# Moving modulation sums, partition sums and a gelu in a one-core hybrid mixer and expert kernel

## The chip, the cores and the metric

One core of one Trainium2 chip runs the whole program. The metric is device time in microseconds from the start to the end of one execution, the lower the better. The time before is 1646.16 us, the median of 3 runs (1645.67 to 1648.39).

## The reference, cut to what matters

One layer over 1024 latent tokens and 256 context tokens of width 1024, in float32. Modulation vectors come from the conditioning vector; four of the six are needed late (gain 1, shift 2, scale 2, gain 2):

```
mod_x = silu(c) @ w_mod + b_mod          # six vectors of 1024
hx = rmsnorm(x, norm1_g) * (1 + sc1x) + sh1x
u, v, xx, g = split(hx @ w_in)           # 512 columns each
rec = gelu(g) * (recurrence of xx, both directions)
sgu = gelu(u) * (spatial mix, per 128 positions, of rmsnorm(gelu(v)))
x = x + g1x * (concat(sgu, rec) @ w_out)
hx2 = rmsnorm(x, norm2_g) * (1 + sc2x) + sh2x
x = x + g2x * expert_choice_ffn(hx2, w_router, w1, w3, w2)   # 16 experts, 128 tokens each
out = rmsnorm(x, final_g)
```

## The kernel before, in words

Every float32 matmul is done as three matmuls on operands split into a rounded part (`hi`, copied by ACT) and its rest (`lo`, subtracted by DVE). The program order written in the file is the order of each engine's queue, and of the load queue of SP.

The stages in order: modulation vectors and x transposed (up to line 502); the recurrence (631 to 680); v and the spatial gate (830 to 875); the output projection with the second norm and the router, tile by tile of 128 tokens (1069 to 1164); selection of tokens by sorting (1168 to 1205); 16 experts (1320 to 1378); the last norm.

**Late modulation vectors.** `mod_rows` (line 396) adds one row block of `w_mod` (128 rows by 1024 columns, 512 KB) times the conditioning value into an accumulator on DVE (line 402 for the first of a vector, line 404 for the other seven). Thirty-two such blocks, eight to a vector, pass through a ring of three buffers; each call then issues the load of the block three further on (`mod_load`, line 389, on SP), which may write only when DVE has read that buffer. `mod_cols` (line 408) sums the accumulator over the 128 partitions with 16 thin matmuls (line 412; the trace counts 16 for 8 written ones) and DVE adds the bias (line 413). The order of vectors is gain 1, scale 2, shift 2, gain 2. The accumulator and the ring lie in two of the twelve 1 MB buffers that the expert weights use later.

**v.** `v_mm(t, h)` (line 754) is 24 matmuls of 256 columns. Tiles 0 to 3 do half 0 first and half 1 in the loop of line 849; tiles 4 to 7 do both in the loop of line 865. `v_evac` (line 766) is a gelu and four squares with row sums on ACT. `v_norm` (line 774) needs the sums of four tiles and scales those tiles on DVE. `spatial_mm` (783) multiplies by the spatial weights on PE, `spatial_ew` (788) applies gain, bias and u on DVE.

**w_out.** Four 1 MB loads in two halves (`load_wo`, 807) through two buffers; `scale_wo` (815) multiplies by gain 1 on DVE, `split_wo` (822) makes `hi` on ACT and `lo` on DVE. Half 1 meets the recurrence, half 0 the spatial gate. The loads of half 0 wait until the subtractions of half 1 have read their buffers.

**Output tiles.** `out_mm(t, h)` (921) is 24 matmuls of 512 columns into two PSUM banks. Before the loop of line 1075, `row_bcast` (732) spreads scale 2 and shift 2 over the partitions: eight transposes on PE for each vector, in two banks each. There are eight PSUM banks, handed out again in about the order in which they come free. In the loop, for tile t: the softmax of the router for t-2, the residual and norm for t-1, `out_mm(t)`, the transposes of `router_t(t-1)` (990), `fill(20)` (941: sorting steps on DVE, where there are any), the next spatial tile, the router product for t-1.

**Expert weights.** `load_next` (84) issues 1 MB loads on SP ahead of use; the first use is at line 1150, behind output tile 7.

Of the kernel before, what the change touches and what calls it, by code (L numbers as in the profile page):

```python
# [11 lines left out]
AF = mybir.ActivationFunctionType  # L12
# [33 lines left out]
def hybrid_layer(ctx, tc, x, c, ctxt, c_ctx, w_mod, b_mod, norm1_g, norm2_g, w_in, sgu_g, sgu_w,  # L46
# [3 lines left out]
    V, A, PE, G = nc.vector, nc.scalar, nc.tensor, nc.gpsimd  # L50
# [19 lines left out]
    def bank(shape, name, small=0):  # L70
        return banks[small].tile(shape, F32, name=name, tag="bk")

    def raw(shape, dt, name):
        return rawp.tile(shape, dt, name=name, tag="raw")

    def raw2(shape, dt, name):
        n = shape[1] // 2
        return Two([raw([shape[0], n] + shape[2:], dt, name) for _ in range(2)], n)
# [5 lines left out]
    def load_next(n=1, queue=nc.sync):  # L84
        for _ in range(n):
            which, w, e, u = pieces.pop(0)
            q, h = divmod(u, 2)
            r = 4096 // w.shape[2]
            t = raw([P, 2048], F32, "raw")
            src = w[e, q * P * r:(q + 1) * P * r, :].rearrange("(p k) f -> p (k f)", p=P)  # L90
            queue.dma_start(t, src[:, h * 2048:(h + 1) * 2048])
            units.append(((which, e, u), t))
# [296 lines left out]
    def mod_load():  # L389
        n = nload[0]  # L390
        if n < len(todo):
            g, k = todo[n]
            nc.sync.dma_start(ring[:, n % 3], w_mod[k * P:(k + 1) * P, (2 + g) * D:(3 + g) * D])
            nload[0] += 1

    def mod_rows(cnt=1):
        for _ in range(cnt):
            n = ndone[0]
            k = todo[n][1]
            macc, row = ring[:, 3], ring[:, n % 3]  # L400
            if k == 0:
                V.tensor_scalar(macc, row, cs[:, k, 0:1], None, op0=OP.mult)
            else:
                V.scalar_tensor_tensor(macc, row, cs[:, k, 0:1], macc, op0=OP.mult, op1=OP.add)  # L404
            ndone[0] += 1
            mod_load()

    def mod_cols():
        g = todo[ndone[0] - 1][0]
        p = bank([P, 8, 2], "pm")  # L410
        for j in range(8):
            PE.matmul(p[:, j], ring[:, 3, j * P:(j + 1) * P], ones, start=True, stop=True)
        V.tensor_tensor(mcol[:, g], p[:, :, 0], prmT[:, 32 + 8 * g:40 + 8 * g], op=OP.add)
# [92 lines left out]
    uT = pu.tile([P, 4, S], F32, name="uT")  # L506
# [225 lines left out]
    def row_bcast(dst, col, view=lambda p: p):  # L732
        for h in range(2):
            p = bank([P, 512], "rb")
            for j in range(4):
                PE.transpose(p[:, j * P:(j + 1) * P],
                             col[:, 4 * h + j:4 * h + j + 1].to_broadcast([P, P]), ident)
            A.activation(dst[h] if isinstance(dst, list) else dst[:, h * 512:(h + 1) * 512], view(p), AF.Copy)  # L738
# [15 lines left out]
    def v_mm(t, h):  # L754
        if h == 0:
            PV[t] = bank([P, 512], "pv")
        hi, lo = hxT[t // 4]
        ts = slice((t % 4) * P, (t % 4 + 1) * P)
        o = PV[t][:, h * 256:(h + 1) * 256]
        for k in range(8):  # L760
            wh, wl = wv[h][k]
            PE.matmul(o, hi[:, k, ts], wh, start=(k == 0), stop=False)
            PE.matmul(o, hi[:, k, ts], wl, start=False, stop=False)
            PE.matmul(o, lo[:, k, ts], wh, start=False, stop=(k == 7))

    def v_evac(t):
        p = PV.pop(t)
        A.activation(gv[:, t], p, AF.Gelu_apprx_tanh)
        junk = psp.tile([P, 512], F32, name="junk2", tag="bk")
        for h in range(4):  # L770
            A.activation(junk[:, h * P:(h + 1) * P], gv[:, t, h * P:(h + 1) * P], AF.Square,
                         accum_out=vst[:, 0, 4 * t + h:4 * t + h + 1])
# [34 lines left out]
    def load_wo(h):  # L807
        return [(k, load_wo2(h, k)) for k in (0, 2)]
# [6 lines left out]
    def scale_wo(h, ts):  # L815

        for k, t in ts:
            for n in range(2):
                v = t[:, :, n * 512:(n + 1) * 512]
                V.tensor_tensor(v, v, g1row[n][:, None, :].to_broadcast([P, 2, 512]), op=OP.mult)  # L820

    def split_wo(h, ts):
        wo[h] = (raw2([P, 4, D], F32R, "woh"), raw2([P, 4, D], F32R, "wol"))
        hi, lo = wo[h]
        for k0, t in ts:
            for k in range(2):
                A.activation(hi[:, k0 + k], t[:, k], AF.Copy)
                V.tensor_sub(lo[:, k0 + k], t[:, k], hi[:, k0 + k])
# [19 lines left out]
    wor1 = load_wo(1)  # L848
    for t in range(4):
        v_mm(t, 1)  # L850
        if t == 0:
            mod_cols()
        if t == 1:
            scale_wo(1, wor1)
        v_evac(t)
        mod_rows(1)
    V.scalar_tensor_tensor(a2c, mcol[:, 2], 1.0, prmT[:, 96:104], op0=OP.add, op1=OP.mult)
    split_wo(1, wor1)
    wor0 = load_wo(0)
    mod_rows(4)  # L860
    for b in range(4):
        A.activation(uT[:, b], uT[:, b], AF.Gelu_apprx_tanh)
    A.preload_act_table_set("natural_log_exp_and_others")
    v_norm(0)
    for t in range(4, 8):
        for h in range(2):
            v_mm(t, h)
        v_evac(t)
        if t == 5:
            scale_wo(0, wor0)  # L870
        if t == 6:
            mod_cols()
    for t in range(3):
        spatial_mm(t)
    spatial_ew(0)
# [26 lines left out]
    def x_load(t):  # L902
        XR[t] = pe_.tile([P, D], F32, name="xr", bufs=2)
        nc.sync.dma_start(XR[t], x[t * P:(t + 1) * P])

    x_load(0)
    x_load(1)
    load_next(2)
    affs = tv[:, :, :, 1]

    groups = ((0,), (1, 2), (3, 4), (5,), (6, 7))
# [9 lines left out]
    def out_mm(t, h, ks=range(4), ns=(0, 1)):  # L921
        ts = slice(t * P, (t + 1) * P)
        if t not in PW:
            PW[t] = [bank([P, 512], "pw") for _ in range(2)]
        yh, yl = (recT[0][:, :, ts], recT[1][:, :, ts]) if h else YH[t]
        pw = PW[t]
        wh, wl = wo[h]
        for k in ks:
            st_, en = h == 1 and k == 0, h == 0 and k == 3
            for n in ns:  # L930
                PE.matmul(pw[n], yh[:, k], wh[:, k, n * 512:(n + 1) * 512], start=st_, stop=False)  # L931
            for n in ns:
                PE.matmul(pw[n], yh[:, k], wl[:, k, n * 512:(n + 1) * 512], start=False, stop=False)  # L933
            for n in ns:
                PE.matmul(pw[n], yl[:, k], wh[:, k, n * 512:(n + 1) * 512], start=False, stop=en)  # L935
# [5 lines left out]
    def fill(n=1):  # L941

        for _ in range(n):
            if fills and not callable(fills[0]) and done2[0] >= fills[0]:
                fills.pop(0)
            if fills and callable(fills[0]):
                fills.pop(0)()
            if fills2:
                fills2.pop(0)()
                done2[0] += 1  # L950
# [39 lines left out]
    def router_t(t, hs=(0, 1)):  # L990
        hx2 = H2[t]
        if t not in HT:
            HT[t] = pe_.tile([P, 8, P], F32, name="hxT2")
        for h in hs:
            p = bank([P, 4, P], "ht")
            for k in range(4):
                PE.transpose(p[:, k], hx2[:, (4 * h + k) * P:(4 * h + k + 1) * P], ident)
            A.activation(HT[t][:, 4 * h:4 * h + 4], p, AF.Copy)
# [68 lines left out]
        q_bitonic(32, m, dst, f)  # L1067

    out_mm(0, 1)
    row_bcast(A2, a2c)  # L1070
    row_bcast([qkp(SH2, 0, 2), qkp(SH2, 2, 2)], mcol[:, 1], lambda p: qpk(p, 0, 2))
    out_mm(1, 1)
    out_mm(0, 0)
    spatial_mm(3)
    for t in range(1, 8):
        if t > 1:
            router_sm(t - 2)
        if t == 2:
            q_sort(0, LS[0])
        if t in (4, 6):  # L1080
            i = t // 2 - 1
            q_sort(i, L1)
            q_merge(LS[1 - i % 2], L1, LS[i % 2])
        norm2_a(t - 1)
        if t + 2 < 8:
            spatial_ew(t + 2)
        if t == 7:
            break
        if t > 1:
            out_mm(t, 1, (0, 1))  # L1090
            router_w(t - 2)
            out_mm(t, 1, (2, 3))
        norm2_b(t - 1)
        y_split(t + 1)
        out_mm(t, 0)
        x_load(t + 1)
        if t == 1:
            spatial_mm(t + 3)
        router_t(t - 1)
        fill(20)  # L1100
        if t == 5:
            load_next(2)
        if t > 1 and t + 3 < 8:
            spatial_mm(t + 3)
        router_mm(t - 1)
# [404 lines left out]
```

## Time and profile before

| | |
|---|---|
| median of 3 runs | 1646.16 us |
| the profiled execution | 1644.65 us |
| its span, first to last instruction | 1642.6 us |
| mean granted TensorE clock | 0.967 of full |
| PE busy | 1537.4 us, 94% |
| DVE busy | 1385.6 us, 84% |
| ACT busy | 1090.2 us, 66% |
| POOL busy | 143.2 us, 9% |
| the chain that ended last, by engine | PE 69%, DVE 13%, DMA 7%, ACT 7%, issue 4% |

A timeline row gives the start in us from the start of the span, the duration, the engine, the source line, the operation, what is written and read, and how many instructions are merged in the row (xN). Brackets at the end hold the time for which the engine had been idle ahead of it, and what released it. SP rows are issues of loads and stores; an issue that lasts long was waiting. A clock of 1.00 is 2.4 GHz, 0.50 is 1.2 GHz.

### The profile page before, as it was taken

Reading aid. Unit: us, or ns where it says so; the run is one execution under the profiler, and the core shown is the slowest. Engines: PE = TensorE matmul, PEld = TensorE weight load, DVE = VectorE, ACT = ScalarE, POOL = GpSimd, SP = SyncE. Lnnn points to the kernel's source line nnn. Section 1 sums busy time; section 2 is a strip of 40 time slices with the busy share of each in tenths; the row PEclk is TensorE's granted clock in tenths of the full one; section 3 lists DMA queues with packets and bytes.
Section 4 is the critical chain, followed back from the end, with each engine's and each line's share of the span. In section 5 each row is a group of like instructions: output and inputs, shape, how many; then the busy total and the mean of one; then the engine's idle time right before and its main releaser. Section 6 shows DMA issues by size and latency. Waiting matters only on the chain.

```text
span 1642.6 us, 19121 instructions
## 1 busy us (share of the span) xinstructions
PE 1537.4 (94%) x7288; PEld 1263.9 (77%) x7288; DVE 1385.6 (84%) x1321; ACT 1090.2 (66%) x990; POOL 143.2 (9%) x126
## 2 busy tenths in 40 slices
PE   5899997989939999999999999999999999999996
PEld 2687777878727888888888888888888888887784
DVE  6669687667875998989989899898988989898897
ACT  6576652632336778687777777768777786777873
POOL 2311121000000000100101000010000101001002
PEclk8999998999959999999999999999999999999998
DMA  9010147333566999999999999999999999999855
GB/s 383 28 36 29 65 154 253 134 128 116 214 268 239 366 384 385 376 360 387 381 373 391 367 378 369 388 383 378 371 364 388 380 382 381 357 388 382 317 188 205
DMA packets 85947, 485.30 MB, mean 295 GB/s; under 512 B 11224, under 2 KB 20064, under 8 KB 35680
## 3 DMA queue, kind: packets, MB, share of 16 engines
q1 hardware_dynamic: 80896, 466.72, 73.9%
q0 software_dynamic: 4864, 17.34, 4.1%
q8 instruction: 57, 0.93, 0.2%
q14 instruction: 34, 0.28, 0.0%
q10 hardware_dynamic: 96, 0.03, 0.0%
HBM read 463.61 MB, written 20.45 MB: 295 GB/s over the span
## 4 chain that ended last, share of the span: by engine, by line
PE 69%; DVE 13%; DMA 7%; ACT 7%; issue 4%; POOL 1%; SPq 0%; DVEq 0%; POOLq 0%; ACTq 0%
PE h L1257 11%; PE h L1261 11%; PE h L1259 11%; PE ye L1303 7%; PE ye L1300 7%; PE ye L1306 7%; DMA raw<-in_w_dram 3%; ACT hi L107 3%; DVE lo L109 3%; DMA ring<-in_w_mod_dram 2%; PE pw L931 2%; PE pw L933 2%; PE pw L935 2%; PE hp L1284 2%; DVE sg L1278 1%
## 5 line engine op out<-in xcount | busy, mean ns | idle before, releaser
L109 DVE TENSOR_TENSOR lo<-raw,hi 128x2048 fp32r<-128x2048 f32 x383 | 870.7, 2291 | 123.7 <-ACT hi L107 120.1
L107 ACT ACTIVATE hi<-raw 128x2048 fp32r<-128x2048 f32 x384 | 737.1, 1921 | 223.4 <-PE h L1261 158.2
L1257 PE MATMUL h<-hi,xth 128*128 128x512 f32 x1024 | 293.1, 400 | 3.6 <-ACT sg L1268 1.3
L1259 PE MATMUL h<-lo,xth 128*128 128x512 f32 x1024 | 280.3, 390 | 1.9 <-DVE lo L109 1.9
L1261 PE MATMUL h<-hi,xtl 128*128 128x512 f32 x1024 | 280.1, 390 | 0.0
L1257 PEld LDWEIGHTS h<-hi,xth 128*128 128x128 f32 x1024 | 188.1, 189 | 50.7 <-DVE sg L1278 12.5
L1259 PEld LDWEIGHTS h<-lo,xth 128*128 128x128 f32 x1024 | 192.7, 188 | 42.8 <-DVE lo L109 2.8
L1261 PEld LDWEIGHTS h<-hi,xtl 128*128 128x128 f32 x1024 | 192.6, 188 | 40.7
L1300 PE MATMUL ye<-hi,hth 128*128 128x512 f32 x512 | 157.9, 390 | 0.0
L1303 PE MATMUL ye<-lo,hth 128*128 128x512 f32 x512 | 157.8, 389 | 0.0
L1306 PE MATMUL ye<-hi,htl 128*128 128x512 f32 x512 | 157.7, 389 | 0.0
L1316 POOL DMA_INDIRECT x2d<-ye,ix x15 | 50.1, 3338 | 790.5 <-DVE ye L1313 790.5
L1306 PEld LDWEIGHTS ye<-hi,htl 128*128 128x128 f32 x512 | 96.1, 188 | 20.1
L1303 PEld LDWEIGHTS ye<-lo,hth 128*128 128x128 f32 x512 | 96.0, 188 | 20.2 <-DVE lo L109 0.3
L1300 PEld LDWEIGHTS ye<-hi,hth 128*128 128x128 f32 x512 | 95.8, 188 | 19.6
L1268 ACT ACTIVATE sg<-h 128x512 f32<-128x512 f32 x64 | 69.9, 1111 | 0.1
L1287 ACT ACTIVATE hth<-hp 128x512 fp32r<-128x512 f32 x64 | 35.0, 596 | 42.3 <-PE hp L1284 42.3
L404 DVE SCALAR_TENSOR_TENSOR ring<-ring,cs 128x1024 f32<-128x1024 f32 x28 | 41.4, 1479 | 14.0 <-DMA ring<-in_w_mod_dram 13.4
L377 PE MATMUL pu<-hxh,wh 128*128 128x512 f32 x128 | 50.8, 397 | 2.6 <-ACT g1row L738 2.6
L1235 POOL DMA_INDIRECT xe<-hx2d,ix x16 | 17.1, 1068 | 400.2 <-DVE gate L1230 238.5
L379 PE MATMUL pu<-hxl,wh 128*128 128x512 f32 x128 | 50.9, 398 | 0.0
L378 PE MATMUL pu<-hxh,wl 128*128 128x512 f32 x128 | 50.8, 397 | 0.0
(346 smaller groups left out, 1910.7 us busy)
## 6 DMA issues: line engine op xcount, KB each, us to landing
raw<-in_w_dram SPq DMA_DIRECT2D x383, 1024.0 KB, 7.3
ring<-in_w_mod_dram SPq DMA_DIRECT2D x32, 512.0 KB, 4.9
wmod<-in_w_mod_dram SPq DMA_DIRECT2D x8, 1024.0 KB, 10.5
wraw<-in_w_in_dram SPq DMA_DIRECT2D x6, 1024.0 KB, 12.1
xh<-in_x_dram SPq DMA_DIRECT2D x4, 1024.0 KB, 15.6
wor<-in_w_out_dram SPq DMA_DIRECT2D x4, 1024.0 KB, 7.8
xr<-in_x_dram SPq DMA_DIRECT2D x8, 512.0 KB, 4.2
x2d<-xr SPq DMA_DIRECT2D x8, 512.0 KB, 2.6
```

The costliest lines, as they stand in the source:

```text
L107: A.activation(hi, s, AF.Copy)
L109: eng.tensor_tensor(lo, s, hi, op=OP.subtract)
L377: PE.matmul(p, w[0][:, k], act[0][:, k], start=(k == 0), stop=False)
L378: PE.matmul(p, w[1][:, k], act[0][:, k], start=False, stop=False)
L379: PE.matmul(p, w[0][:, k], act[1][:, k], start=False, stop=(k == 7))
L1257: PE.matmul(pt[b], hi[:, k], wh[:, b * 512:(b + 1) * 512], start=(k == 0), stop=False)
L1259: PE.matmul(pt[b], hi[:, k], wl[:, b * 512:(b + 1) * 512], start=False, stop=False)
L1261: PE.matmul(pt[b], lo[:, k], wh[:, b * 512:(b + 1) * 512], start=False, stop=(k == 7))
L1268: A.activation(s.rearrange("t j p -> t p j"), pt[b].rearrange("t (p j) -> t p j", j=4), AF.Silu)
L1300: PE.matmul(pt[n], hi[:, j], wh[:, j2 * 1024 + n * 512:j2 * 1024 + n * 512 + 512], start=st_, stop=False)
L1303: PE.matmul(pt[n], hi[:, j], wl[:, j2 * 1024 + n * 512:j2 * 1024 + n * 512 + 512], start=False, stop=False)
L1306: PE.matmul(pt[n], lo[:, j], wh[:, j2 * 1024 + n * 512:j2 * 1024 + n * 512 + 512], start=False, stop=en)
```

## The change

In the first v loop the partition sums of shift 2 move from behind tile 0 to behind tile 3, and the scaling of w_out half 1 from behind tile 1 to behind those sums. Of the eight sums for gain 2, one stood behind each of tiles 0 to 3 and four behind the split of half 1; three now stand ahead of that scaling, three in output tile 1 and two in output tile 2. The gelu of u moves ahead of the split of half 1. The partition sums of gain 2 move from v tile 6 to output tile 3. The first two loads of expert weights move from ahead of the output tiles to output tile 3, since the ring keeps its two buffers until then. `out_mm(1, 1)` moves ahead of the two `row_bcast`.

```
--- before.py
+++ after.py
@@ -848,18 +848,15 @@
     wor1 = load_wo(1)
     for t in range(4):
         v_mm(t, 1)
-        if t == 0:
-            mod_cols()
-        if t == 1:
-            scale_wo(1, wor1)
         v_evac(t)
-        mod_rows(1)
+    mod_cols()
+    mod_rows(3)
+    scale_wo(1, wor1)
     V.scalar_tensor_tensor(a2c, mcol[:, 2], 1.0, prmT[:, 96:104], op0=OP.add, op1=OP.mult)
+    for b in range(4):
+        A.activation(uT[:, b], uT[:, b], AF.Gelu_apprx_tanh)
     split_wo(1, wor1)
     wor0 = load_wo(0)
-    mod_rows(4)
-    for b in range(4):
-        A.activation(uT[:, b], uT[:, b], AF.Gelu_apprx_tanh)
     A.preload_act_table_set("natural_log_exp_and_others")
     v_norm(0)
     for t in range(4, 8):
@@ -868,8 +865,6 @@
         v_evac(t)
         if t == 5:
             scale_wo(0, wor0)
-        if t == 6:
-            mod_cols()
     for t in range(3):
         spatial_mm(t)
     spatial_ew(0)
@@ -905,7 +900,6 @@
 
     x_load(0)
     x_load(1)
-    load_next(2)
     affs = tv[:, :, :, 1]
 
     groups = ((0,), (1, 2), (3, 4), (5,), (6, 7))
@@ -1067,9 +1061,9 @@
         q_bitonic(32, m, dst, f)
 
     out_mm(0, 1)
+    out_mm(1, 1)
     row_bcast(A2, a2c)
     row_bcast([qkp(SH2, 0, 2), qkp(SH2, 2, 2)], mcol[:, 1], lambda p: qpk(p, 0, 2))
-    out_mm(1, 1)
     out_mm(0, 0)
     spatial_mm(3)
     for t in range(1, 8):
@@ -1097,8 +1091,12 @@
         if t == 1:
             spatial_mm(t + 3)
         router_t(t - 1)
+        if t < 3:
+            mod_rows((3, 2)[t - 1])
+        if t == 3:
+            mod_cols()
         fill(20)
-        if t == 5:
+        if t in (3, 5):
             load_next(2)
         if t > 1 and t + 3 < 8:
             spatial_mm(t + 3)
```

## Rows read from the trace of the kernel before

**Rows 1.** The page's fifth part, the first group of matmuls of the expert stage.

```profile
L1257 PE MATMUL h<-hi,xth 128*128 128x512 f32 x1024 | 293.1, 400 | 3.6 <-ACT sg L1268 1.3
```

**Rows 2.** Timeline of PE: the four waits between 256 and 345 us, and output tile 0.

```profile
279.00 3.55 PE L412 MATMUL pm<-ones,ring 128*128 128x2 f32 x16 [9.66 <-DVE ring L404]
...
313.23 2.36 PE L412 MATMUL pm<-ones,ring 128*128 128x2 f32 x16 [3.83 <-DVE vst L209]
...
335.03 0.49 PE L931 MATMUL pw<-woh,rech 128*128 128x512 f32 x1 [1.21 <-DVE gv L791]
...
338.18 0.60 PE L931 MATMUL pw<-woh,rech 128*128 128x512 f32 x1 [2.65 <-DVE gv L791]
...
345.12 0.62 PE L931 MATMUL pw<-woh,yh 128*128 128x512 f32 x2
```

**Rows 3.** Timeline of PE: three shorter waits earlier in the run.

```profile
66.15 0.50 PE L459 MATMUL px<-hxl,wh 128*128 128x512 f32 x1 [1.77 <-DVE hxl L370]
...
142.42 0.39 PE L377 MATMUL px<-hch,wh 128*128 128x256 f32 x1 [2.25 <-DVE xb L541]
...
222.42 1.92 PE L412 MATMUL pm<-ones,ring 128*128 128x2 f32 x16 [1.09 <-DVE ring L404]
```

**Rows 4.** Busy time by stretch, PE alone (columns: stretch, length, PE busy, granted clock, DMA share, GB/s).

```profile
66.00:72.00 6.00, 5.44 (x29) 1.00 0.02 4
143.00:148.00 5.00, 5.00 (x27) 0.66 0.51 163
279.00:287.00 8.00, 8.00 (x37) 0.50 0.85 316
287.25:309.40 22.15, 22.15 (x195) 1.00 0.71 247
```

**Rows 5.** Timeline of DVE between v and output tile 0.

```profile
290.05 2.36 DVE L820 TENSOR_TENSOR wor<-wor,g1row 128x1024 f32<-128x1024 f32 x2 [0.19 <-DMA wor<-in_w_out_dram]
...
292.33 3.92 DVE L404 SCALAR_TENSOR_TENSOR ring<-ring,cs 128x1024 f32<-128x1024 f32 x3
...
311.80 1.28 DVE L404 SCALAR_TENSOR_TENSOR ring<-ring,cs 128x1024 f32<-128x1024 f32 x1 [6.88 <-DMA ring<-in_w_mod_dram]
...
316.95 4.62 DVE L820 TENSOR_TENSOR wor<-wor,g1row 128x1024 f32<-128x1024 f32 x4
...
328.71 4.63 DVE L828 TENSOR_TENSOR wol<-wor,woh 128x1024 fp32r<-128x1024 f32 x4 [2.00 <-ACT woh L827]
```

**Rows 6.** Timeline of ACT between v and output tile 0.

```profile
275.10 0.58 ACT L768 ACTIVATE gv<-pv 128x512 f32<-128x512 f32 x1
...
299.17 3.89 ACT L862 ACTIVATE uT<-uT 128x1024 f32<-128x1024 f32 x4
...
314.98 0.60 ACT L768 ACTIVATE gv<-pv 128x512 f32<-128x512 f32 x1
...
317.22 0.58 ACT L768 ACTIVATE gv<-pv 128x512 f32<-128x512 f32 x1
...
326.32 1.28 ACT L876 ACT_TABLE_LOAD   x1
```

**Rows 7.** Timeline of SP: issues of the w_out and w_mod loads.

```profile
279.92 0.94 SPq L812 DMA_DIRECT2D wor<-in_w_out_dram  x2
...
283.44 13.16 SPq L393 DMA_DIRECT2D ring<-in_w_mod_dram  x4
```

**Rows 8.** Timeline of DVE and PE in output tiles 1 to 3.

```profile
361.19 0.17 DVE L1008 TENSOR_REDUCE ss<-pl 128x1 f32<-128x16 f32 x1 [2.87 <-PE pl L1004]
...
376.11 0.15 DVE L1008 TENSOR_REDUCE ss<-pl 128x1 f32<-128x16 f32 x1
...
382.82 1.28 DVE L985 SCALAR_TENSOR_TENSOR hx<-tm,ss,SH2row 128x1024 f32<-128x1024 f32 x1
...
390.37 0.17 DVE L1008 TENSOR_REDUCE ss<-pl 128x1 f32<-128x16 f32 x1 [5.66 <-PE pl L1004]
...
386.71 1.03 PE L997 MATMUL ht<-ident,hx 128*128 128x128 f32 x8
```

More of the change, by code (lines that the diff above doesn't have):

```diff
@@ L850, in hybrid_layer @@
         v_mm(t, 1)
[L851 to L854, printed above, removed]
         v_evac(t)
-        mod_rows(1)
+    mod_cols()
+    mod_rows(3)
+    scale_wo(1, wor1)
     V.scalar_tensor_tensor(a2c, mcol[:, 2], 1.0, prmT[:, 96:104], op0=OP.add, op1=OP.mult)
+    for b in range(4):
+        A.activation(uT[:, b], uT[:, b], AF.Gelu_apprx_tanh)
     split_wo(1, wor1)
     wor0 = load_wo(0)
-    mod_rows(4)
-    for b in range(4):
-        A.activation(uT[:, b], uT[:, b], AF.Gelu_apprx_tanh)
     A.preload_act_table_set("natural_log_exp_and_others")
@@ L870, in hybrid_layer @@
             scale_wo(0, wor0)
-        if t == 6:
-            mod_cols()
     for t in range(3):
@@ L907, in hybrid_layer @@
     x_load(1)
-    load_next(2)
     affs = tv[:, :, :, 1]
@@ L1069, in hybrid_layer @@
     out_mm(0, 1)
+    out_mm(1, 1)
     row_bcast(A2, a2c)
     row_bcast([qkp(SH2, 0, 2), qkp(SH2, 2, 2)], mcol[:, 1], lambda p: qpk(p, 0, 2))
-    out_mm(1, 1)
     out_mm(0, 0)
@@ L1099, in hybrid_layer @@
         router_t(t - 1)
+        if t < 3:
+            mod_rows((3, 2)[t - 1])
+        if t == 3:
+            mod_cols()
         fill(20)
-        if t == 5:
+        if t in (3, 5):
             load_next(2)
```

## The prediction

> **What bounds the kernel now.** I read the page first: PE is busy for 94% of the span, and the expert stage, by far the longest, runs its matmuls with next to no idle time: 3.6 us ahead of 1024 of them [rows 1]. So whatever starts the experts earlier ends the kernel earlier by as much, and the change is worth what it does to the time at which they start. Then I read PE's timeline between v and output tile 0, for rows with an idle time in brackets. There are four: 9.66 us ahead of the partition sums of shift 2, which stand in PE's queue behind v tile 0 and need DVE's last row sum; 3.83 us ahead of those of gain 2; 1.21 and 2.65 us ahead of output tile 1, whose two banks wait for the spatial gate's DVE work [rows 2]. Last, the stretches: after the 9.66 us the granted clock is 0.50 for 8 us, and in undisturbed v work it is 1.00 at 195 matmuls in 22.15 us, 0.1136 us each [rows 4]. The sum below goes against this execution: 1644.65 us, of which the span is 1642.6. It stands 1.5 us under the median of 1646.16, and I take the difference to the median at the end. A measurement of this kernel can tell about 0.2%, 3.3 us, from no change.
>
> **The first v loop on PE.** Tile 0's half 1 ends at 279.00 - 9.66 = 269.34. With the sums gone from behind it, three more halves of 24 matmuls at 0.1136 us follow: until 277.5. The last row sum of shift 2 is not moved, so the partition sums start at 279.0 as before, now after 1.5 us of idle time instead of 9.66. They cost 1.92 us at full clock after a wait of 1.09 [rows 3], against 3.55 at half clock [rows 2]. PE is free at 280.9, with v tiles 0 to 3 behind it; before, tiles 1 to 3 still stood ahead. Tiles 4 to 7 are 192 matmuls, 21.8 us: 302.7, with no sums of gain 2 between them (3.83 idle, 2.36 busy and half clock after it [rows 2] go). The first three spatial tiles, 24 matmuls at about the same pace, end at 305.4, output tile 0's recurrent half (24 matmuls of twice the columns, 5.45 us by estimate) at 310.9, and output tile 1's, now ahead of the broadcasts, at 316.3. Three of the four broadcast banks (0.46 us each, by the pace) bring PE to 317.7.
>
> **The DVE and ACT chain beside it.** The three row sums that now stand ahead of the w_out scaling take 3.92 us [rows 5] from 281 on; they are over when w_out arrives, since the scaling waits for its load until 290.05 [rows 5], and SP issued that load at 279.92, ahead of anything the change moves [rows 7]. The price is therefore nothing; without that cover it would be 3.92. Scaling ends at 292.4, as before. Now the split follows at once: DVE subtracts from 292.6 for 4.63 us, to 297.2, where before 3.92 us of row sums came first. The gelu of u (3.89 us) runs on ACT from 275.10 + 4 x 2.24 = 284.1 to 288.0 [rows 6], in time that ACT spends waiting for the scaling, so it too costs nothing; if w_out came 2 us earlier, it would show. Behind the split DVE had four more row sums, the last after 6.88 us of waiting for its load, ending at 311.80 + 1.28 = 313.08 [rows 5]; the normalization of v followed. Now it follows at 297.2, 15.9 us earlier. From there I copy the old distances: the next gelu of v starts 314.98 - 313.08 = 1.90 later, at 299.1; four evacuations at 2.24 end at 308.1 [rows 6]; the scaling of half 0 starts 316.95 - 313.08 later, at 301.1, and takes 4.62, so it is no longer last. From the table load at 326.32 to PE's release at 338.18 lie 11.86 us of ACT and DVE work that the change leaves alone [rows 2, 6]: 308.1 + 11.86 = 319.9. This release now frees the bank of the fourth broadcast transpose instead of output tile 1's second bank.
>
> **Output tile 0.** PE stands at 317.7 and is released at 319.9: a wait of 2.2 us, then 0.46 for the last transposes, so the spatial half of tile 0 starts at 320.4, against 345.12 [rows 2]: 24.7 us earlier.
>
> **The clock after that wait.** A wait of 1.77 us left the clock at 1.00, one of 2.25 us was followed by 5 us at 0.66 [rows 3, 4]. 2.2 lies next to the second, so I charge it: 5 x 0.34 = 1.7 us. Bounds: nothing, and the 8 us at 0.50, 4.0 us. The Trainium skill, "TensorE: Matmul & The Clock Gate", section on HAM oscillation, speaks against the change here: short idle gaps between groups of matmuls, from cycling PSUM banks, can make the clock swing. By that rule all three gaps that the change leaves would cost; the rows bear it out for one of them, and its time is the first rival's below.
>
> **Output tiles 1 to 3.** Three row sums of 3.92 us come into tile 1, where DVE had waited 2.87 us for PE [rows 8]: 1.05 late. Two more (two thirds of 3.92, 2.61) come into tile 2, where DVE went from sorting into the softmax at 376.11 without a wait [rows 8]: 3.66 late in all. The normalized tile 2, ready at 382.82 + 1.28 = 384.10, is then ready at 387.76, and PE's transposes, at 386.71, wait 1.05. Behind them stand the partition sums of gain 2, 1.92 us [rows 3]. Together PE is 2.97 us later, say 3.0. In tile 3 DVE waited 5.66 us for the router product [rows 8], so from there PE sets the pace again and the delay does not grow. Bounds: the 1.92 alone, and all five sums on the path (6.53 + 1.92 = 8.45). The loads that these sums issue (blocks 27 to 29 behind w_out half 1, 30 and 31 in tile 1) have a tile's time or more to land. The two expert loads now pass behind eleven loads and stores on SP (nine of output tiles 0 to 4, and blocks 30 and 31); SP waits for the partition sums ahead of them, but the next store comes after those, and the first reader is behind tile 7. POOL gets nothing. I charge nothing for them; the bound is their own time, 2 MB at 316 GB/s [rows 4], 6.6 us, if that cover were gone.
>
> **The sum.** -24.7 + 1.7 + 3.0 = -20.0: the profiled execution would take 1624.65, and the median 1646.16 - 20.0 = 1626.2 us.
>
> **The rivals.** First, **every short gap drops the clock**: besides the charged one, the 1.5 us gap ahead of shift 2 and the 1.05 in tile 3. At 1.7 us each the first disappears in the 2.2 us wait, the second adds 1.7: 1627.9. At 4.0 each: 4.0 - 2.2, 2.3 and 4.0 more, 1634.3. Against it: the 1.77 gap. I put it at 1631. Second, **the row loads delay w_out**: blocks 28 and 29 (1 MB) now load beside half 1. If they share the bandwidth of 316 GB/s instead of queueing, the chain is 3.3 us late: 1629.5. One load between them did not show it before [rows 5, 7]. Third, **the wait moves instead of going**: the sums of shift 2 need a bank, and if theirs is one that v tile 3's evacuation holds, they wait until 284.1, run at half clock for 3.55 us and leave 4.45 us more of it. v then ends at 284.1 + 3.55 + 2.2 + 21.8 = 311.7, PE comes to the last broadcast at 326.7, behind ACT's release at 325.7, and tile 0's spatial half starts near 327.2: 6.8 us less gain, without the charged 1.7, 1631.3. Fourth, **DVE sets the pace in tiles 1 to 3**: 8.45 instead of 3.0, 1631.7. Fifth, the other side, **the clock stays low**: if the gap at 277.5 takes the clock to 1.2 GHz until tile 0's spatial half, 36.8 us of PE work (280.9 to 317.7) double, that half starts at 355.0, 9.9 later than now, and with the 3.0 the time is 1659.1. It decides from about 48 us of low clock on: 20.0 + 1.7 + 2.2 of lost work, twice that of clock. The longest such stretch of busy PE that I read is 8 us [rows 4], which speaks against it. The Trainium skill, same page, section "Seeing it yourself", reports a clock stuck low for over 50 us; no row here shows that.
>
> **How the numbers follow.** Forecast 0.55, first rival 0.13, second 0.09, third 0.08, fourth 0.07, fifth 0.03; 0.05 for what I don't see, mostly small. The low end takes back the charges: 1.7 of clock, 1.05 in tile 3, and the 2.2 us wait if the bank order differs: 1621.2. The high end takes in the second to fourth rivals and most of the first: 1633. Left out are the fifth, the worst of the first and part of the unseen, about 0.15. Faster by over 0.2%: 0.95; within: 0.02; slower: 0.03.
>
> **What would show it.** Right: no wait above 2 us on PE between v tile 0 and tile 7, the sums of shift 2 after some 1.5 us, the normalization of v near 297, a wait of about 2 us ahead of the last broadcast, the spatial half of tile 0 near 320 to 321, about 1 us of wait ahead of the transposes in tile 3, and all later rows some 20 us earlier. Wrong: a w_out half 1 that lands after 292, a wait on ACT ahead of the sums, a granted clock of 0.5 in v tiles 4 to 7, new waits of PE on DVE in tiles 1 to 3, or an expert stage that starts earlier and doesn't end earlier.

## The result, and the profile after

The changed kernel takes **1626.83 us** (median of 4 runs, 1620.83 to 1628.22) against 1645.91 beside it: ratio **0.9884**, 95% interval 0.9865 to 0.9902. Twelve more runs of it in two later comparisons have medians of 1626.71 and 1626.81. The forecast was 1626.2. The profiled execution of the changed kernel is the fastest of its four, 1620.83 us with a span of 1618.7; why it stands 6 us under its own median is one thing that the experiments had to find out.

Transposes of the router stand one output tile behind the rows that they hold. Below, "tile 0's transposes" are those of tile 0's rows, which run in output tile 1; "the transposes in output tile 3" hold tile 2's rows. TensorE's timeline of the changed kernel, from v to output tile 3:

```profile
259.28 2.32 PE L412 MATMUL pm<-ones,ring 128*128 128x2 f32 x16 [1.51 <-ACT wvh L704]
...
278.83 1.84 PE L412 MATMUL pm<-ones,ring 128*128 128x2 f32 x16
...
317.68 0.60 PE L736 MATMUL rb<-ident,mcol 128*128 128x128 f32 x4
319.62 0.65 PE L736 MATMUL rb<-ident,mcol 128*128 128x128 f32 x4 [1.33 <-DVE gv L791]
320.02 0.71 PE L925 MATMUL pw<-woh,yh 128*128 128x512 f32 x2
...
362.62 1.07 PE L991 MATMUL ht<-ident,hx 128*128 128x128 f32 x8 [0.72 <-DVE hx L979]
363.52 1.84 PE L412 MATMUL pm<-ones,ring 128*128 128x2 f32 x16
365.23 1.14 PE L786 MATMUL ss<-gg,gv 128*128 128x128 f32 x8
366.20 1.86 PE L998 MATMUL pl<-wr,hxT 128*128 128x16 f32 x16
```

Against [rows 2]: the 9.66 us ahead of the partition sums of shift 2 (L412, second line) are gone, with no bracket left at all, and so are the 3.83 us ahead of those of gain 2, which now stand in output tile 3. Output tile 1 no longer waits twice for its banks; one wait of 1.33 us stands ahead of the last broadcast. The spatial half of output tile 0 starts at 320.02 instead of 345.12, 25.1 us earlier. New are 0.72 us ahead of the transposes in output tile 3. Of the 25.1 us, 18.6 are the release that TensorE waits for (338.18 in [rows 2], 319.62 now). The other 6.5 stand behind it: from there to the spatial half it was 6.94 us, with output tile 1's second bank in between, and is now 0.40. The granted clock in v, and behind the wait ahead of the broadcast:

```profile
260.00:268.00 8.00, 8.00 (x44) 0.57 0.60 176
279.00:287.00 8.00, 8.00 (x70) 1.00 0.92 333
287.00:303.00 16.00, 16.00 (x139) 1.00 0.74 276
320.00:328.00 8.00, 8.00 (x42) 1.00 0.04 15
```

(stretch, length, busy, matmuls, granted clock, DMA share, GB/s). The stretch at 279 had 37 matmuls at 0.50 [rows 4]; it now has 70 at 1.00. The first of these stretches says why the sums of shift 2 have no wait at all in this execution. Its clock had fallen to 0.50 behind the 1.51 us ahead of the partition sums of scale 2 (the first line of the timeline), which the change does not move, so TensorE came to the sums of shift 2 at 278.83, 1.3 us later than the forecast's 277.5, when VectorE's last row sum (278.38) was done. VectorE's timeline, the counterpart of [rows 5] and, from 333 on, of [rows 8]:

```profile
281.78 1.28 DVE L404 SCALAR_TENSOR_TENSOR ring<-ring,cs 128x1024 f32<-128x1024 f32 x1 [0.25 <-DMA ring<-in_w_mod_dram]
283.61 1.28 DVE L404 SCALAR_TENSOR_TENSOR ring<-ring,cs 128x1024 f32<-128x1024 f32 x1 [0.55 <-DMA ring<-in_w_mod_dram]
287.40 4.81 DVE L820 TENSOR_TENSOR wor<-wor,g1row 128x1024 f32<-128x1024 f32 x4 [2.50 <-DMA wor<-in_w_out_dram]
292.20 4.62 DVE L828 TENSOR_TENSOR wol<-wor,woh 128x1024 fp32r<-128x1024 f32 x4
296.75 0.17 DVE L209 TENSOR_SCALAR vst<-vst 128x16 f32<-128x16 f32 x1
...
333.24 3.92 DVE L404 SCALAR_TENSOR_TENSOR ring<-ring,cs 128x1024 f32<-128x1024 f32 x3
337.08 0.17 DVE L1002 TENSOR_REDUCE ss<-pl 128x1 f32<-128x16 f32 x1
...
354.49 0.15 DVE L1002 TENSOR_REDUCE ss<-pl 128x1 f32<-128x16 f32 x1
```

The row sums are over by 284.9, and VectorE still waits 2.50 us for w_out: they are covered. The first group's norm (L209) starts at 296.75. In tiles 1 and 2 the router's softmax (L1002) follows without a bracket, so VectorE is the later one there.

Where the time came from, by the start of the same work in the two profiled executions: tile 0's transposes 357.90 to 332.92 (25.0 us earlier), those in output tile 3 386.71 to 362.62 (24.1), tile 7's 452.98 to 430.36 (22.6), the first expert's transposes 489.40 to 466.77 (22.6), the end of the span 1642.6 to 1618.7 (23.9). Through the experts it stays between 22.6 and 22.9; the last 1.0 us appears in the final stage, which the change leaves alone.

### The profile page after: what moved, and what is told of

It reads as the page before. It is cut to its first block, busy times and chain, and to the rows that moved or that the text cites. A ratio compares the mean times of both kernels' runs of the same rounds, so it can differ in the third digit from the quotient of the medians.

```text
span 1618.7 us, 19117 instructions
## 1 busy us (share of the span) xinstructions
PE 1527.6 (94%) x7288; PEld 1254.8 (78%) x7288; DVE 1383.8 (85%) x1321; ACT 1089.6 (67%) x990; POOL 143.6 (9%) x126
## 4 chain that ended last, share of the span: by engine, by line
PE 66%; DVE 16%; ACT 7%; DMA 6%; issue 4%; POOL 1%; SPq 0%; DVEq 0%; POOLq 0%; ACTq 0%
PE h L1257 12%; PE h L1259 12%; PE h L1255 12%; PE ye L1301 7%; PE ye L1298 7%; PE ye L1304 7%; ACT hi L107 3%; DMA raw<-in_w_dram 3%; DVE lo L109 2%; PE hp L1282 2%; DVE ring L404 1%; DMA ring<-in_w_mod_dram 1%; DVE sg L1276 1%; PE xp L1243 1%; DMA ctx_sb<-in_ctx_dram 1%
## 5 line engine op out<-in xcount | busy, mean ns | idle before, releaser
L1298 PEld LDWEIGHTS ye<-hi,hth 128*128 128x128 f32 x512 | 95.8, 188 | 19.7
```

The source lines that it names most:

```text
L1298: PE.matmul(pt[n], hi[:, j], wh[:, j2 * 1024 + n * 512:j2 * 1024 + n * 512 + 512], start=st_, stop=False)
```

## The experiments

The theory under test was the forecast's own, and each expectation names its rival. The first four kernels ran on one chip, where the kernel before took 1644.77 us (15 runs); the next four on another (1644.11, 9 runs); the last four, in a later comparison, on the first again (1645.38, 11 runs).

**The changed kernel again** (no edit).

> The changed kernel once more, beside the others on one chip. Theory (the spatial half of output tile 0 starts 24 to 25 us earlier, of which 3 are given back in tiles 1 to 3): 19 to 22 us under the kernel before, ratio 0.987 to 0.989, the waits of PE at 1.3 us ahead of the last broadcast and 0.7 us in tile 3 as in its first profile. Rival (most of the gain of the profiled execution came from the expert stage by chance): under 15 us.

Measured: 1626.71 us (6 runs, 1620.51 to 1630.67), ratio 0.9888 (0.9863 to 0.9913); profiled at 1627.46, span 1625.3. That is 18.1 us under the kernel before, a little less than the 19 to 22 expected, and more than the rival's 15. This profile is the one to hold against the faster one:

```profile
278.49 1.92 PE L412 MATMUL pm<-ones,ring 128*128 128x2 f32 x16 [1.00 <-ACT junk L771]
...
320.67 0.65 PE L736 MATMUL rb<-ident,mcol 128*128 128x128 f32 x4 [1.88 <-DVE gv L791]
...
365.28 1.06 PE L991 MATMUL ht<-ident,hx 128*128 128x128 f32 x8 [0.76 <-DVE hx L979]
366.18 1.85 PE L412 MATMUL pm<-ones,ring 128*128 128x2 f32 x16
367.88 1.14 PE L786 MATMUL ss<-gg,gv 128*128 128x128 f32 x8
368.86 3.02 PE L998 MATMUL pl<-wr,hxT 128*128 128x16 f32 x16
```

The waits are the same within 1 us, but the router product (last line) takes 3.02 instead of 1.86: the clock fell while it ran. In windows of this execution (columns as above):

```profile
279.00:284.00 5.00, 5.00 (x32) 0.66 0.95 266
321.00:324.00 3.00, 3.00 (x11) 0.59 0.00 0
368.00:380.00 12.00, 12.00 (x53) 0.72 0.63 256
```

Each has 1.00 in the faster execution. From the last broadcast to tile 0's transposes this execution takes 14.89 us instead of 13.30 (1.6 more), from the transposes in output tile 3 to those in tile 4 19.70 instead of 16.50 (3.2 more), and from those in tile 5 to those in tile 6, where the clock falls once more (403 to 407), 15.90 instead of 14.24 (1.7). That is 6.5 us. It was 1.05 us behind already at the last broadcast, and 0.9 come back later, so the spans differ by 6.6. In this pair the gap is mostly the granted clock, which falls to 0.50 (1.2 GHz) for a few us at places where TensorE has just waited, or runs its narrow matmuls (128 columns or fewer, where the wide ones have 256 or 512). The third profile, further down, differs from the first mainly for another reason.

**Only the shift-2 part** (row sums of gain 2 back behind the split, five of them, their partition sums back in v tile 6, and the first weight loads back ahead of the output tiles).

```diff
     wor0 = load_wo(0)
+    mod_rows(5)
...
+        if t == 6:
+            mod_cols()
...
-        if t < 3:
-            mod_rows((3, 2)[t - 1])
-        if t == 3:
-            mod_cols()
```

> The changed kernel with the row sums of gain 2 back ahead of the normalization of v (five behind the split), their partition sums back at v tile 6 and the first weight loads back ahead of the output tiles. Theory: the normalization of v waits for the last row block again, which loads behind w_out half 0, and starts near 306 instead of 297; PE waits some 8 us at v tile 6; the spatial half of tile 0 starts some 10 us later than in the changed kernel, less the 3 us that tiles 1 to 3 no longer give back: 6 to 9 us above the changed kernel, 12 to 15 under the kernel before. Rival (the first wait of PE was the whole gain, and where the sums of gain 2 stand does not matter): within 3 us of the changed kernel.

Measured: 1633.64 us (7 runs), ratio 0.9940 (0.9918 to 0.9962): 6.9 us over the changed kernel, 11.1 under the kernel before.

```profile
306.75 3.55 PE L412 MATMUL pm<-ones,ring 128*128 128x2 f32 x16 [9.97 <-DVE vst L209]
```

The wait of [rows 2] ahead of these sums does not just stay, it grows from 3.83 to 9.97 us. TensorE now reaches them 12.6 us earlier (296.78 for 309.40), and the row sums that they need are over only 6.5 us earlier (306.60 for 313.08).

**Only the gain-2 part** (partition sums of shift 2 and the scaling back inside the first v loop).

```diff
     for t in range(4):
         v_mm(t, 1)
+        if t == 0:
+            mod_cols()
+        if t == 1:
+            scale_wo(1, wor1)
         v_evac(t)
-    mod_cols()
     mod_rows(3)
-    scale_wo(1, wor1)
```

> The changed kernel with the partition sums of shift 2 back behind v tile 0 and the scaling of w_out half 1 back behind tile 1. Theory: PE's first wait of some 9.7 us and its 8 us at half clock are back, the normalization of v starts near 301, v tile 7 ends near 315, the spatial half of tile 0 starts near 330 against 320: 9 to 11 us above the changed kernel, 9 to 12 under the kernel before; so the two parts alone add up to more than the whole, since each removes a wait that the other's chain also covers. Rival (additive parts): the changed kernel's gain less that of the sums of shift 2 alone, some 6 to 8 us under the kernel before.

Measured: 1636.22 us (8 runs), ratio 0.9949 (0.9930 to 0.9967): 9.5 over the changed kernel, 8.6 under the kernel before.

```profile
277.40 3.54 PE L412 MATMUL pm<-ones,ring 128*128 128x2 f32 x16 [7.09 <-DVE ring L404]
```

The long wait is back, and the spatial half of tile 0 starts at 329.54. The two parts "alone" gain 11.1 and 8.6 us, together 19.7, and both at once 18.1. That does not show that they add up: both kernels keep the two other moves (output tile 1's half and the gelu), so 19.7 counts these twice. What can be compared is the loss when one move is undone: 6.9 and 9.5 here and 7.5 in the next kernel, 23.9 in all, more than the 18.1 of the whole. That points to moves that are worth more together than apart. Whether the two sums' moves by themselves add up was not measured: no kernel has the two other moves alone.

**Output tile 1's recurrent half behind the broadcasts**, where it was before.

```diff
     out_mm(0, 1)
-    out_mm(1, 1)
     row_bcast(A2, a2c)
     row_bcast([qkp(SH2, 0, 2), qkp(SH2, 2, 2)], mcol[:, 1], lambda p: qpk(p, 0, 2))
+    out_mm(1, 1)
     out_mm(0, 0)
```

> The changed kernel with the recurrent half of output tile 1 back behind the two broadcasts. Theory: its banks wait for the spatial gate again, until 319.6 for the second one, so its 5.5 us come behind that wait instead of ahead of it, and the longer wait may drop the clock: 5 to 7 us above the changed kernel. Rival (the order of these does not matter, since PE waits for the spatial gate in either): within 1 us of the changed kernel.

Measured: 1634.21 us (7 runs), ratio 0.9938 (0.9914 to 0.9962), 7.5 over the changed kernel, a little more than the 5 to 7 expected.

```profile
317.19 0.49 PE L925 MATMUL pw<-woh,rech 128*128 128x512 f32 x1 [3.37 <-DVE gv L791]
...
320.34 0.80 PE L925 MATMUL pw<-woh,rech 128*128 128x512 f32 x1 [2.65 <-DVE gv L791]
```

Both waits of [rows 2] are back, 6.0 us of them, and in this execution the clock is at 0.50 behind them (318 to 325). This half tile, 24 matmuls, is work that needs nothing from the spatial gate, and ahead of the broadcasts it fills the time until the banks come free.

**The gelu of u behind the split.**

```diff
-    for b in range(4):
-        A.activation(uT[:, b], uT[:, b], AF.Gelu_apprx_tanh)
     split_wo(1, wor1)
     wor0 = load_wo(0)
+    for b in range(4):
+        A.activation(uT[:, b], uT[:, b], AF.Gelu_apprx_tanh)
```

> The changed kernel (about 1626.7 us) with the gelu of u put back behind the split of half 1 of w_out, all else as changed. Theory: ScalarE reaches the exponent of the first group's norm about 2.5 us later than in the changed kernel (its four gelu instructions, 4 x 3.89 us, no longer stand in the time in which it waits for the scaled rows), and the norm, the release of the junk buffer and with them the spatial half of output tile 0 shift by the same: +2.5 to +4.2 us, 1629 to 1631. Rival: ScalarE has enough idle time ahead of the release, the place of the gelu is worth nothing: 1626 to 1627.5, inside 0.2%.

Measured: 1628.59 us (5 runs), ratio 0.9911 (0.9894 to 0.9928). By medians 1.8 us over the changed kernel, whose runs were on another chip; the intervals overlap, so the size is not settled by the times, and the median lies between the ranges of theory and rival. (The four gelu instructions take 3.89 us together [rows 6], not each, as the expectation has it.) The mechanism shows on VectorE, whose second step of the norm (L214) waits for ScalarE:

```profile
297.49 0.17 DVE L209 TENSOR_SCALAR vst<-vst 128x16 f32<-128x16 f32 x1
300.61 0.17 DVE L214 TENSOR_TENSOR vst<-vst 128x16 f32<-128x16 f32 x1 [2.95 <-ACT vst L211]
```

In the first two profiles of the changed kernel this wait is 0.53: 2.4 us are added to the chain that releases output tile 0. From this step to the last broadcast it takes 22.2 us in all three profiles, so the delay reaches output tile 0 whole.

**Row sums where VectorE waits** (two in tile 1, three in tile 3; partition sums and the weight loads in tile 4).

```diff
-        if t < 3:
-            mod_rows((3, 2)[t - 1])
-        if t == 3:
+        if t in (1, 3):
+            mod_rows(2 if t == 1 else 3)
+        if t == 4:
             mod_cols()
...
-        if t in (3, 5):
+        if t in (4, 5):
```

> The changed kernel with two row sums in output tile 1 and three in tile 3 (where VectorE waits for TensorE) instead of three and two in tiles 1 and 2, and the gain-2 partition sums with the first two weight loads one tile later, in tile 4. Theory A: the drops of TensorE's granted clock to 0.50 that some executions show behind the partition sums come from the run of narrow matmuls alone, wherever it stands among other narrow ones: they stay, and only some 0.7 us of VectorE's work leaves the path: 1625.5 to 1626.5. Theory B: they need a wait of 0.7 us just ahead of it, which the move takes away: the drops behind tile 3 go and 4 us with them, 1622 to 1623.

Measured: 1625.07 us (4 runs), ratio 0.9893 (0.9875 to 0.9912). Inconclusive: the median lies beside theory A, but in the profile the clock stays up behind the sums (377.50, without a wait) and falls one tile later (VectorE's and TensorE's timelines):

```profile
379.38 0.17 DVE L413 TENSOR_TENSOR mcol<-pm,prmT 128x8 f32<-128x8 f32 x1 [4.83 <-PE pm L412]
...
394.81 1.06 PE L991 MATMUL ht<-ident,hx 128*128 128x128 f32 x8 [1.72 <-DVE hx L979]
```

Neither theory said that. The first row has a cause for the wait: VectorE's add that reads the sums stood 4.83 us waiting for them, and behind it VectorE has no more idle time until it is late with these rows.

**Sums amid wide matmuls** (as the last, but between the halves of tile 4's product).

```diff
+            if t == 4:
+                mod_cols()
             out_mm(t, 1, (2, 3))
```

> As rows_in_waits, but the gain-2 partition sums stand between the two halves of output tile 4's matmuls, with wide matmuls on both sides, and not beside the narrow transposes. Theory A (narrow work beside narrow work lowers the granted clock): no drop to 0.50 at tiles 3 and 4, 1622 to 1623.5, some 3.5 us below rows_in_waits. Rival (place does not matter): as rows_in_waits, and the difference of the two is within 1 us.

Measured: 1622.99 us (4 runs), ratio 0.9878 (0.9859 to 0.9897), 2.1 under the last kernel where 3.5 was expected. No wait and no fall of the clock stand at tiles 3 and 4; one of 3 us is left in tile 5. The 2.1 us cannot be put down to the neighbours of the sums alone: here VectorE's add finds them ready (370.19, no wait), and the 4.83 us for which it waited in the last kernel are gone too.

**Sums where TensorE waits** (behind tile 7's product).

```diff
     out_mm(7, 0, (1, 2, 3), (1,))
+    mod_cols()
     router_sm(6)
```

> As rows_in_waits, but the gain-2 partition sums stand behind the matmuls of output tile 7, where TensorE waits some 4 us for VectorE, and the first weight loads of the experts go out in tile 5 and behind tile 7. Theory: TensorE pays neither the 1.9 us of the sums nor a drop of the clock in tiles 3 and 4: 1620 to 1621.5, some 6 us below the changed kernel. Rival: the gain-2 vector comes late for the gather rows, or the loads come late for the first expert, and 1625 us or more stays.

Measured: 1625.16 us (4 runs), ratio 0.9881 (0.9864 to 0.9897). The theory missed, and neither reason of the rival was the cause: from the last transposes to the first expert's it takes 36.2 us, in the changed kernel 36.4. TensorE ran the sums in its idle time, but VectorE's add that reads them waited in order:

```profile
430.32 0.17 DVE L413 TENSOR_TENSOR mcol<-pm,prmT 128x8 f32<-128x8 f32 x1 [3.95 <-PE pm L412]
...
431.75 0.67 DVE L951 TENSOR_TENSOR xr<-pw,xr 128x512 f32<-128x512 f32 x1
...
435.75 1.97 PE L991 MATMUL ht<-ident,hx 128*128 128x128 f32 x8 [5.46 <-DVE hx L1152]
```

The last tile's residual (L951) stands behind that add; TensorE's last transposes then wait 5.46 us for it instead of 4.05, and from tile 6's transposes to these it takes 13.7 us instead of 10.7.

**The add late** (only TensorE's part stays there).

```diff
-    mod_cols()
+    add3 = mod_cols(False)
     router_sm(6)
...
+    add3()
     nc.sync.dma_start(hx2d[7 * P:], hx2)
```

> As sums_in_waits, but only the partition sums of gain 2 on TensorE stand behind output tile 7's matmuls; VectorE's add of 128x8 that reads them is issued after the last normalized rows of tile 7. Theory: in sums_in_waits that add, which waited 3.95 us for TensorE, held up the last tile's residual and norm behind it on VectorE; with it gone from there the step from tile 6's transposes to tile 7's second half falls from 13.7 us to about 10.7 and the time by some 3 us, to 1621 to 1623. Rival: the last tile is set by the matmuls and not by the add, and it stays at 1625.

Measured: **1619.60 us** (5 runs, 1616.95 to 1620.71), ratio 0.9843 (0.9823 to 0.9863).

```profile
426.00 1.85 PE L412 MATMUL pm<-ones,ring 128*128 128x2 f32 x16
430.22 1.97 PE L992 MATMUL ht<-ident,hx 128*128 128x128 f32 x8 [2.38 <-DVE hx L1153]
```

The wait is 2.38 us, 1.67 less than the 4.05 of the changed kernel: the sums run inside it. From tile 6's transposes to these it takes 10.7 us again, so the theory holds for the step. The gain over the kernel with the add in place, 5.6 us by the medians of two chips, is more than the 3 expected. In the two profiles 3.1 us of it arise in that step; 2.5 stand already at tile 6's transposes (422.01 and 419.56), ahead of anything that differs between the two programs.

**The broadcast of shift 2 behind the spatial half.**

```diff
-    row_bcast([qkp(SH2, 0, 2), qkp(SH2, 2, 2)], mcol[:, 1], lambda p: qpk(p, 0, 2))
     out_mm(0, 0)
+    row_bcast([qkp(SH2, 0, 2), qkp(SH2, 2, 2)], mcol[:, 1], lambda p: qpk(p, 0, 2))
```

> As sums_add_late, with the broadcast of shift 2 behind the spatial half of output tile 0 instead of ahead of it. Theory: the wait of 0.7 to 2.5 us ahead of the last broadcast (for a bank that VectorE's spatial gate frees) goes, since the spatial half of tile 0 finds its operands ready some 4 us earlier: 1 to 2 us less than sums_add_late. Rival: the broadcast then comes late for the first normalized rows, a wait of the same size stands ahead of tile 0's transposes, and the time is the same within 1 us.

Measured: 1619.45 us (4 runs), ratio 0.9852 (0.9828 to 0.9875): no gain. The wait ahead of the broadcast is gone (the profile of the kernel with the add late has none there either; its clock was at 0.50 from 280 to 286, and TensorE came late), and one of 1.63 us stands ahead of tile 0's transposes, as the rival had it, though not for the broadcast: VectorE, which normalizes these rows, has the gate, the second norm of v and the residual ahead of them, with no idle time over 0.7 us from 318 on, and starts on them at 330.27.

```profile
331.61 0.66 PE L992 MATMUL ht<-ident,hx 128*128 128x128 f32 x4 [1.63 <-DVE hx L980]
```

**The shift-2 sums amid v tile 4.**

```diff
+    v_mm(4, 0)
     mod_cols()
```

> As sh2_behind, with the partition sums of shift 2 between the two halves of v tile 4 instead of between v tiles 3 and 4. Theory: narrow matmuls right behind a wait of 1 to 2 us are what lowers the granted clock to 0.50 for 4 to 7 us in most executions at this place; behind half a tile of wide matmuls they do not: 1.5 to 2 us less than sh2_behind where VectorE and ScalarE don't set the release of output tile 0, 0 to 1 where they do; together 1618 to 1621. Rival: the three row sums behind these partition sums come 1.5 us later and delay the scaling of w_out: 1 us more.

Measured: 1620.33 us (4 runs), ratio 0.9850 (0.9828 to 0.9873): within 1 us of the two before. A wait of 1.65 us now stands ahead of wide matmuls, and the clock stays at 1.00 from 278 to 290 (timeline, and a window):

```profile
280.22 0.39 PE L763 MATMUL pv<-wvh,hxh 128*128 128x256 f32 x1 [1.65 <-ACT junk L772]
```

```profile
278.00:290.00 12.00, 10.35 (x89) 1.00 0.92 302
```

The kernel before it in this list kept 1.00 there too, however, behind a wait of 1.24 us and narrow sums. So the theory about the clock was not tested by this pair. That a full clock in v gains little fits the two profiles of the changed kernel above: the 22.2 us from the norm to the last broadcast are the same with the clock at 1.00 in v and with a fall there.

**The changed kernel a third time**, beside the three last ones.

> The changed kernel once more, as the measure for the three others on the same chip: 1625.5 to 1628.

Measured: 1626.81 us (6 runs, 1623.39 to 1632.38), ratio 0.9894 (0.9870 to 0.9917), profiled at 1628.34. In tile 3 its clock fell as in the second profile (TensorE's timeline, and a window of it):

```profile
324.41 0.65 PE L736 MATMUL rb<-ident,mcol 128*128 128x128 f32 x4 [1.54 <-DVE gv L791]
...
367.44 1.06 PE L991 MATMUL ht<-ident,hx 128*128 128x128 f32 x8 [0.77 <-DVE hx L979]
368.34 1.84 PE L412 MATMUL pm<-ones,ring 128*128 128x2 f32 x16
370.04 1.59 PE L786 MATMUL ss<-gg,gv 128*128 128x128 f32 x8
371.42 3.43 PE L998 MATMUL pl<-wr,hxT 128*128 128x16 f32 x16
```

```profile
369.00:380.00 11.00, 11.00 (x53) 0.69 0.82 302
```

Its span is 7.5 us longer than the first profile's. Of this 3.2 arise here, but 4.8 stand already at the last broadcast (324.41 and 319.62). Most of that is older than anything that the change moves: the clock stays at 0.50 until 56 us instead of 49 and falls again at 70, and at the sums of scale 2 this execution is 2.9 us behind (262.13 and 259.28).

The kernel with the add late beats it by 7.2 us on the same chip, and the kernel before by 25.8.

## Why the prediction was right

**The bound and the main term.** The forecast gain of 20.0 us came as 19.1 in the first comparison and as 18.1 and 18.6 in the later ones. What starts the experts earlier ends the kernel earlier: the first expert starts 22.6 us earlier, the end comes 23.9 earlier, and the matmul groups of [rows 1] are unchanged. The term of -24.7 us for the spatial half of tile 0 came as -25.1, with each link near its place: norm at 296.75 for 297.2, release at 319.6 for 319.9, spatial half at 320.02 for 320.4. These are the fastest execution's numbers. In the other two profiles the spatial half starts at 321.08 (24.0 us earlier) and 324.81 (20.3), the last one late from early in the run. The undone parts confirm what the term consists of: without either partition sum's move, or without output tile 1's half ahead of the broadcasts, 6.9 to 9.5 us are lost. (Besides the four waits counted there is a fifth of 0.83 us at 265.89, ahead of four transposes and of everything that the change moves.)

**The steps costed at nothing.** The three row sums ahead of the scaling were covered, as said, by the load of w_out. The gelu of u was free where it stands now and cost 2.4 us of the chain behind the split. The second rival, the row loads delaying w_out, came in small: from the issue of w_out to the start of its scaling it takes 7.9, 9.0 and 8.8 us in the three profiles of the changed kernel against 7.6 before (279.92 to 287.50), so up to 1.4 us where that rival had 3.3.

**The wait ahead of shift 2.** Forecast 1.5 us; none, 1.00 and 2.57 in the three profiles, the last over the 2 us that the forecast allowed. That there was none in the first is an accident of that execution: TensorE was late itself, behind the fall of its clock at 260. The third rival said that it would be a bank of v's evacuation. In the second profile the releaser is indeed ScalarE, at the bank that its squares of v write to (`junk`), but the wait is 1.0 us long and does not last until 284.1: the rival's price was wrong. In the third it is VectorE's row sum.

**Tiles 1 to 3.** Forecast 1.05 us of wait and 1.92 of sums, 3.0 in all. Measured at full clock: the step into tile 3 is 15.41 us instead of 14.53, and the step out of it 16.50 instead of 14.66: 0.9 and 1.8, 2.7 in all. The fourth rival (VectorE carries the whole 6.5 us on) did not come, and neither did the fifth: no fall of the clock between v and tile 0's spatial half lasted over 7 us in these three profiles.

**The clock, the step that was mis-sized.** I charged 1.7 us once, behind the wait ahead of the last broadcast. There the clock fell in one of three profiles (after 1.88 us, not after 1.33 or 1.54), for 1.6 us. What the sum left out is tile 3: the 16 narrow matmuls of gain 2 now stand between two other narrow groups behind a short wait, and in two of the changed kernel's three profiles the clock then fell to 0.50, which cost 3.2 us. Over all six profiles of kernels with these sums there, it fell in four (3.2 and 4.8 us); in none of the eight other profiles, the one of before among them, did it fall in that step. The clock falls elsewhere without these sums too, for example from 434 to 437 us in the kernel before. My first rival had the right event, but tied to gaps alone and for 1.7 to 4.0 us. That the sum came out near the median is in this part luck: the charge that was not due in two profiles of three and the missing one that was due in two of three are of like size. With no fall of the clock between 270 and 430 us the execution took 1620.8 and with four of them 1627.5; the one with two took 1628.3, since it came late into v, and these three times alone give no price of a fall.

The Trainium skill, "TensorE: Matmul & The Clock Gate", section "A second HAM failure mode: psum-queue depth-cycling", says that frequent short idle gaps between groups of matmuls make the clock swing between its two levels. The traces agree that it swings (0.50 and 1.00) where gaps of 0.7 to 2.6 us stand, and add that the size of a gap does not decide: 0.76 us ahead of the same three narrow groups was followed by 0.50 in two profiles (the second of the changed kernel, and output tile 1's half behind the broadcasts) and by 1.00 in a third (the gelu behind the split).

**What stays open.** Whether narrow matmuls alone, or only behind a wait, lower the clock: the kernel made to tell showed a fall one tile later, behind a wait that its own add had caused. And of the 7.2 us by which the kernel with the add late beats the changed kernel, 2.7 are the waits and sums of tiles 2 and 3. The other 4.5 are not shown. The fall in tile 3 (3.2 us where it comes) is gone, but the profile of the faster kernel has two falls of its own (280 to 286, and 338 to 341), and of the 8.2 us between the two profiles made beside each other 3.5 stand already at the sums of scale 2 (262.13 and 258.68), ahead of every edit.

## What to carry to other kernels

Put a reduction where the engine that feeds it is early, and put independent wide work ahead of anything that needs a freed bank: here the moves took 18 us off. When a small reduction is parked in one engine's idle time, park its reader too: an add of 0.17 us that waited in order held VectorE for 3.95 us and undid such a move, and with the add issued later the move paid. Narrow matmuls cost least in a wait that exists anyway; beside other narrow ones, behind a new wait, they were followed by a fall of the clock in four profiles of six.

## What the runs showed of the hardware that was not expected

One kernel on one chip gives 1620.5 to 1632.4 us. Of the difference between two profiled executions of it (6.6 us of span), 6.5 us arise in the three steps in which the granted clock fell to 0.50, for 3 to 7 us each. The size of a wait did not decide: ahead of the last broadcast the clock fell behind 1.88 and 2.11 us (the gelu behind the split), and not behind 1.33, 1.54 or 2.50 us (the sums amid wide matmuls). The profiled executions of the changed kernel lie 7.5 us apart, so a single one of each version cannot tell two apart here that differ by less.
